# Which feed-forward prepares the rounding remainders of two mixers' weights

## The chip, the cores and the metric

The kernel runs on one core of a Trainium2 chip. The metric is the device time of one execution in microseconds, as the median of several. The core has a matrix engine (PE, TensorE), two elementwise engines (DVE is VectorE, ACT is ScalarE), a general one (POOL, GpSimd) and a queue that only issues transfers here (SP, SyncE). The trace lists when each instruction ran, what it waited for and which clock the matrix engine was granted.

## The reference

A sequence of 512 positions of width 1024 passes through seven layers with a residual sum, each on an RMS-normed input. In short:

```python
x = x + 0.5 * swiglu(rms(x), w_ffn1)                # f1
x = x + mixer1(rms(x))                              # m1: recurrence, window attention
x = x + 0.5 * swiglu(rms(x), w_ffn2)                # f2
x = x + rms(even_mixer(rms(x), w_in_even, w_out_even))   # e: short convolution, dilated attention
x = x + rms(conv_ffn(rms(x), w_up0, w_down0))       # f3
x = x + rms(odd_mixer(rms(x), w_in_odd, w_out_odd)) # o: long convolution, stick-breaking attention
x = x + rms(conv_ffn(rms(x), w_up1, w_down1))       # f4
```

Everything is float32. The even mixer has an input matrix of 1024 x 3072 and an output matrix of 1024 x 1024, the odd one 1024 x 2560 and 1024 x 1024. The feed-forwards have 2816 hidden units, a gate and an up part each; conv_ffn adds a causal convolution of 3 taps on the gate.

## The kernel before

**Three products for one.** The matrix engine reads rounded float32 (`fp32r`). Each weight and each activation is therefore cut in two: `hi`, the value rounded by a cast on ACT, and `lo`, the remainder `raw - hi`, by a subtraction on DVE. `mm3` (L168) makes three matmuls of them: whi*xhi, wlo*xhi, whi*xlo (L170, L171, L172), each 128x128 weights by 512 (or 256) columns. A weight tile of 128x1024 thus gives 24 matmuls.

**How a weight tile comes in.** `wload` (L107) issues one 512 KB transfer into `raw` (3 buffers), casts it to `whi` on ACT (L132) and subtracts on DVE into `wlo` (L139); `whi` and `wlo` have 3 buffers each. Where the source is a `Split` (L37), a pair of DRAM tensors, the subtraction is left out and `wlo` is loaded by a second transfer from the second tensor (L137), issued on SP like the first.

**Who writes that second tensor.** `presplit` (L144) is a generator. Its first step swaps the entry in `ins` for a `Split`; each step handles one tile of 128x1024: load it into one of the 3 `raw` buffers (L151), twice cast a half to a temporary (L155) and subtract in place (L156), then store the tile to DRAM (L157). `ffn` (L418) takes such a generator as `extra=(generator, steps)` and advances it after each of its 22 hidden tiles `j`, so that `steps` steps are spread over the up phase (L455 to L458). For each `j` the up phase has two weight tiles (gate into PSUM kind "m", up into "o"), 48 matmuls, the gate's scaling, optional convolution (L446 to L450), SiLU (L451), the product (L453) and its split (L454). Then comes the down phase (`finish`, L213).

**Stages.** `build` (L1156) runs f1, m1, f2, e, f3, o, f4. Before the change `presplit` of `w_in_odd` (20 tiles) and `w_out_odd` (8 tiles) runs in f2; only the odd mixer reads a `Split`. The even mixer (L866) loads 24 tiles of `w_in_even` and 8 of `w_out_even`, all cut by ACT and DVE. It starts with `begin` (L192), which loads five tiles and runs their products on each half of the columns as soon as that half is normed; then it weaves the projections of four head pairs (`unit`), the short convolution (`gated`) and attention steps (`attention`, L482), and ends with `out_proj` (L965), four of whose eight tiles go to buffers of their own (`oh`, `ol`). In an attention step DVE adds the bias and takes the row maximum (L579), ACT the exponential (L581), DVE the reciprocal and the scaling (L583, L584), PE transposes (L511), ACT and DVE split the result (L514, L515), and PE multiplies by the values (L527).

**What sets the order.** The program is written tile by tile; a planner lays out the order of instructions on each engine beforehand from priorities (program order) and modelled durations, and places the waits. On the chip each queue runs in that fixed order. SP's queue holds every transfer of the kernel: a load that waits for its buffer holds up all loads behind it.

Of the kernel before, what the change touches and what calls it, by code (L numbers as in the profile page):

```python
# [19 lines left out]
KD = D // P  # L20
# [1135 lines left out]
def build(tc, ins, out, stages=STAGES):  # L1156
    with ExitStack() as ctx:
        n = Net(ctx, tc, ins)
        n.out = out
        n.early = stages[0] != "f1"  # L1160
        if n.early:
            n.consts()
        if n.early:
            n.first_prep(PREP[stages[0]])
            n.prep(PREP[stages[0]], WHOLE)
        for s, t in zip(stages, [*stages[1:], "end"]):
            nxt = PREP.get(t, ("end",))
            if s == "f1":
                n.ffn(ins["w_ffn1_gu"], ins["w_ffn1_down"], nxt)
            elif s == "m1":  # L1170
                n.mixer1(nxt)
            elif s == "f2":
                extra = n.chain(n.presplit("w_in_odd"), n.presplit("w_out_odd"))
                n.ffn(ins["w_ffn2_gu"], ins["w_ffn2_down"], nxt, extra=(extra, 28))
                for _ in extra:
                    pass
            elif s == "e":
                n.even(nxt)
            elif s == "f3":
                n.ffn(ins["w_up0"], ins["w_down0"], nxt, conv=("w_fc", "b_fc", 0), post=("norm_g", 3 * KD))  # L1180
            elif s == "o":
                n.odd(nxt)
            elif s == "f4":
                n.ffn(ins["w_up1"], ins["w_down1"], nxt, conv=("w_fc", "b_fc", 1), post=("norm_g", 7 * KD))
# [139 lines left out]
```

## Time and profile before

| | us |
|---|---|
| median of 3 runs | 2469.83 |
| lowest and highest | 2468.75, 2471.17 |
| the profiled execution | 2468.92 |
| its span, first to last instruction | 2467.1 |

Busy time is given per engine over the span. A matmul's printed duration overlaps with the next one's, so that the distance from one start to the next, or the number of matmuls in a stretch, tells more than busy time. In the trace f2 has its up phase until about 1105 us, the even mixer runs from about 1239 to 1490 us, f3 from there to about 1838 us with its up phase until about 1720 us, and the odd mixer from there to about 2110 us.

### The profile page before, as it was taken

Reading aid. Unit: us, or ns where it says so; the run is one execution under the profiler, and the core shown is the slowest. Engines: PE = TensorE matmul, PEld = TensorE weight load, DVE = VectorE, ACT = ScalarE, POOL = GpSimd, SP = SyncE. Lnnn points to the kernel's source line nnn. Section 1 sums busy time; section 2 is a strip of 40 time slices with the busy share of each in tenths; the row PEclk is TensorE's granted clock in tenths of the full one; section 3 lists DMA queues with packets and bytes.
Section 4 is the critical chain, followed back from the end, with each engine's and each line's share of the span. In section 5 each row is a group of like instructions: output and inputs, shape, how many; then the busy total and the mean of one; then the engine's idle time right before and its main releaser. Section 6 shows DMA issues by size and latency. Waiting matters only on the chain.

```text
span 2467.1 us, 32225 instructions
## 1 busy us (share of the span) xinstructions
PE 2401.1 (97%) x12710; PEld 2046.1 (83%) x12710; DVE 1474.5 (60%) x2524; ACT 1129.3 (46%) x1849; POOL 38.8 (2%) x75
## 2 busy tenths in 40 slices
PE   9999999999999999999999999999999879999998
PEld 8888898777777798888988798888898759888887
DVE  5444347888888755553566665554358985655434
ACT  5223236766666544442355554333246556433322
POOL 0000000000000000000000000000001120000000
PEclk9999999999999999999999999999999999999999
DMA  4232333322222256663432222223354313232232
GB/s 151 94 103 92 94 112 119 96 88 88 79 100 84 86 203 213 215 225 98 116 120 90 77 95 77 94 94 98 95 166 152 127 54 136 69 100 97 90 99 92
DMA packets 83560, 276.10 MB, mean 112 GB/s; under 512 B 9328, under 2 KB 14064, under 8 KB 83408
## 3 DMA queue, kind: packets, MB, share of 16 engines
q1 hardware_dynamic: 83408, 274.03, 34.2%
q8 instruction: 100, 1.64, 0.3%
q14 instruction: 52, 0.43, 0.1%
HBM read 257.20 MB, written 16.80 MB: 111 GB/s over the span
## 4 chain that ended last, share of the span: by engine, by line
PE 83%; DVE 10%; ACT 5%; issue 1%; DMA 1%; POOL 0%; SPq 0%; ACTq 0%; DVEq 0%; POOLq 0%
PE psm L172 15%; PE psm L170 15%; PE psm L171 15%; PE pso L170 10%; PE pso L171 10%; PE pso L172 10%; ACT whi L132 1%; DVE wlo L139 1%; DVE pso L1058 1%; PE pst L511 1%; PE pso L527 1%; PE pst L278 1%; PE pst L170 1%; PE pst L172 1%; PE pst L171 1%
## 5 line engine op out<-in xcount | busy, mean ns | idle before, releaser
L132 ACT CAST whi<-raw 128x1024 fp32r<-128x1024 f32 (+3 forms) x402 | 408.4, 1017 | 755.8 <-issue 332.5
L139 DVE TENSOR_TENSOR wlo<-raw,whi 128x1024 fp32r<-128x1024 f32 (+2 forms) x380 | 447.6, 1179 | 311.1 <-ACT whi L132 309.9
L170 PE MATMUL psm<-hh,whi 128*128 128x512 f32 (+1 forms) x1512 | 572.9, 379 | 4.0 <-ACT hh L321 2.8
L171 PE MATMUL psm<-hh,wlo 128*128 128x512 f32 (+1 forms) x1512 | 569.0, 376 | 0.0
L172 PE MATMUL psm<-hl,whi 128*128 128x512 f32 (+1 forms) x1512 | 568.8, 376 | 0.0
L170 PEld LDWEIGHTS psm<-hh,whi 128*128 128x128 f32 x1512 | 285.8, 189 | 53.9 <-ACT hh L321 3.9
L172 PEld LDWEIGHTS psm<-hl,whi 128*128 128x128 f32 x1512 | 285.6, 189 | 49.1 <-DVE hl L322 0.4
L171 PEld LDWEIGHTS psm<-hh,wlo 128*128 128x128 f32 x1512 | 286.4, 189 | 46.0
L170 PE MATMUL pso<-hh,whi 128*128 128x512 f32 (+1 forms) x728 | 272.5, 374 | 0.9 <-ACT whi L132 0.9
L172 PE MATMUL pso<-hl,whi 128*128 128x512 f32 (+1 forms) x728 | 272.3, 374 | 0.0
L171 PE MATMUL pso<-hh,wlo 128*128 128x512 f32 (+1 forms) x728 | 272.2, 374 | 0.2 <-DVE wlo L139 0.2
L171 PE MATMUL psm<-mh,wlo 128*128 128x512 f32 (+1 forms) x506 | 172.4, 341 | 1.6 <-DVE wlo L139 1.6
L172 PE MATMUL psm<-ml,whi 128*128 128x512 f32 (+1 forms) x506 | 172.0, 340 | 0.0
L170 PE MATMUL psm<-mh,whi 128*128 128x512 f32 (+1 forms) x506 | 172.0, 340 | 0.0
L170 PEld LDWEIGHTS pso<-hh,whi 128*128 128x128 f32 x728 | 137.8, 189 | 25.0 <-ACT whi L132 1.1
L172 PEld LDWEIGHTS pso<-hl,whi 128*128 128x128 f32 x728 | 137.7, 189 | 24.6 <-issue 0.5
L171 PEld LDWEIGHTS pso<-hh,wlo 128*128 128x128 f32 x728 | 137.7, 189 | 24.4 <-DVE wlo L139 0.5
L453 DVE TENSOR_TENSOR md<-pso,gp 128x512 f32<-128x512 f32 x84 | 58.1, 692 | 164.2 <-PE pso L172 162.7
L171 PE MATMUL pso<-mh,wlo 128*128 128x256 f32 (+1 forms) x440 | 145.6, 331 | 1.3 <-DVE wlo L139 1.3
L170 PE MATMUL pso<-mh,whi 128*128 128x256 f32 (+1 forms) x440 | 145.8, 331 | 0.3 <-ACT whi L132 0.3
L172 PE MATMUL pso<-ml,whi 128*128 128x256 f32 (+1 forms) x440 | 145.7, 331 | 0.0
L171 PEld LDWEIGHTS psm<-mh,wlo 128*128 128x128 f32 x506 | 96.6, 191 | 12.7 <-DVE wlo L139 2.2
(293 smaller groups left out, 3764.1 us busy)
## 6 DMA issues: line engine op xcount, KB each, us to landing
raw<-w_up SPq DMA_DIRECT2D x88, 512.0 KB, 3.3
raw<-w_ffn_gu SPq DMA_DIRECT2D x87, 512.0 KB, 3.4
raw<-w_in SPq DMA_DIRECT2D x56, 512.0 KB, 3.3
raw<-w_ffn_down SPq DMA_DIRECT2D x40, 512.0 KB, 3.5
raw<-w_in_odd SPq DMA_DIRECT2D x40, 512.0 KB, 3.9
raw<-w_down SPq DMA_DIRECT2D x38, 512.0 KB, 3.5
raw<-w_in_even SPq DMA_DIRECT2D x24, 512.0 KB, 3.5
w_in_odd_lo<-raw SPq DMA_DIRECT2D x20, 512.0 KB, 3.0
```

The lines of the kernel that those rows point to most:

```text
L132: nc.scalar.copy(hi, raw[:, c])
L139: nc.vector.tensor_tensor(out=lo, in0=raw[:, c], in1=hi.bitcast(F32), op=ALU.subtract)
L170: nc.tensor.matmul(out, w[0], x[0], start=start, stop=False)
L171: nc.tensor.matmul(out, w[1], x[0], start=False, stop=False)
L172: nc.tensor.matmul(out, w[0], x[1], start=False, stop=stop)
L278: self.nc.tensor.matmul(st[:, b : b + 1], sq[:, i * P : (i + 1) * P], self.ones[:, 0:1], start=new and i == 0, stop=True, skip_group_check ...
L453: nc.vector.tensor_tensor(out=md, in0=pu, in1=gp, op=ALU.mult)
L511: nc.tensor.transpose(pt[:, i * P : (i + 1) * P], p[:, i * P : (i + 1) * P], self.ident)
L527: nc.tensor.matmul(o[:, q0:q1], V[:, g, a].rearrange("p i d -> p (i d)"), p[:, c], start=first, stop=g == 3 and p is pl, skip_group_check= ...
L1058: nc.vector.scalar_tensor_tensor(t, pad[:, i : i + S], w(i), t, ALU.mult, ALU.add)
```

## The change

`presplit` of the odd mixer's matrices moves from f2 to f3, and f2 now prepares the even mixer's matrices in the same way. The even mixer then reads a `Split`, so its 32 tiles are loaded as two transfers each and are cast on ACT but not subtracted on DVE. f2 advances 32 steps in place of 28, f3 28 in place of none. A loop after f2 that used up what is left of the generator goes; 32 is the number of its tiles (24 + 8), as 28 is for the odd mixer (20 + 8).

```diff
             elif s == "f2":
-                extra = n.chain(n.presplit("w_in_odd"), n.presplit("w_out_odd"))
-                n.ffn(ins["w_ffn2_gu"], ins["w_ffn2_down"], nxt, extra=(extra, 28))
-                for _ in extra:
-                    pass
+                extra = n.chain(n.presplit("w_in_even"), n.presplit("w_out_even"))
+                n.ffn(ins["w_ffn2_gu"], ins["w_ffn2_down"], nxt, extra=(extra, 32))
             elif s == "e":
                 n.even(nxt)
             elif s == "f3":
-                n.ffn(ins["w_up0"], ins["w_down0"], nxt, conv=("w_fc", "b_fc", 0), post=("norm_g", 3 * KD))
+                extra = n.chain(n.presplit("w_in_odd"), n.presplit("w_out_odd"))
+                n.ffn(ins["w_up0"], ins["w_down0"], nxt, conv=("w_fc", "b_fc", 0), post=("norm_g", 3 * KD), extra=(extra, 28))
```

## Rows read from the trace of the kernel before

**Rows 1.** Page, part 1: busy time, share of the span, instructions by engine.
```profile
PE 2401.1 (97%) x12710; PEld 2046.1 (83%) x12710; DVE 1474.5 (60%) x2524; ACT 1129.3 (46%) x1849; POOL 38.8 (2%) x75
```
**Rows 2.** Stretches in f2, f3: length, busy PE, PEld, DVE, ACT, POOL, clock, DMA.
```profile
950.00:1100.00 150.00, 150.00 (x664) 124.20 (x663) 81.00 (x104) 62.81 (x90) 0.00 (x0) 1.00 0.64 221
1550.00:1700.00 150.00, 150.00 (x664) 124.24 (x663) 80.16 (x97) 54.02 (x68) 0.00 (x0) 1.00 0.30 98
```
**Rows 3.** The same view: even mixer between its begin and its tail.
```profile
1250.00:1440.00 190.00, 187.20 (x1004) 157.55 (x1004) 120.71 (x254) 104.81 (x205) 0.13 (x2) 1.00 0.30 98
```
**Rows 4.** PE's waits, 1250 to 1440 us: total us, times, longest.
```profile
PE pst L511 <- DVE l L584: 2.5, 6, 0.6
```
**Rows 5.** DVE's subtractions of weights, 1228 to 1440 us: busy, mean ns.
```profile
L139 DVE TENSOR_TENSOR wlo<-raw,whi 128x1024 fp32r<-128x1024 f32 (+1 forms) x33 | 39.7, 1206 | 16.9 <-ACT whi L132 16.6
```
**Rows 6.** Timelines of DVE, then PE, at an attention step: start us, duration.
```profile
1315.75 1.23 DVE L139 TENSOR_TENSOR wlo<-raw,whi 128x1024 fp32r<-128x1024 f32 x1
...
1318.17 0.39 PE L171 MATMUL psm<-hh,wlo 128*128 128x512 f32 x1
1318.81 0.44 PE L511 MATMUL pst<-ident,l 128*128 128x128 f32 x2 [0.25 <-DVE l L584]
```
**Rows 7.** The chain that ended last, where it passes a subtraction before a transpose.
```profile
1279.15 1.23 DVE wlo L139
...
1352.48 1.23 DVE wlo L139
```
**Rows 8.** Timelines of ACT, then PE, before the other kind of wait.
```profile
1324.22 0.72 ACT L581 ACTIVATE l<-l,m 128x512 f32<-128x512 f32 x1
...
1326.12 0.63 PE L511 MATMUL pst<-ident,l 128*128 128x128 f32 x4 [0.55 <-DVE l L584]
```
**Rows 9.** Page, part 5: the halves that presplit casts and subtracts, 28 steps.
```profile
L156 DVE TENSOR_TENSOR raw<-raw,hi 128x512 fp32r<-128x512 f32 x56 | 36.5, 687 | 41.2 <-ACT hi L155 41.2
L155 ACT CAST hi<-raw 128x512 fp32r<-128x512 f32 x56 | 32.0, 616 | 52.1 <-DMA raw<-w_in_odd 33.1 <-DMA raw<-w_out_odd 19.0
```
**Rows 10.** ACT's waits in f2's up phase, 885 to 1100 us.
```profile
ACT hi L155 <- DMA raw<-w_in_odd: 29.9, 11, 5.6
ACT whi L132 <- DMA raw<-w_ffn_gu: 12.7, 4, 5.2
```
**Rows 11.** Timelines of ACT, then DVE, in f3's up phase: one weight tile.
```profile
1602.24 1.05 ACT L132 CAST whi<-raw 128x1024 fp32r<-128x1024 f32 x1 [1.01 <-PE pso L172]
1603.33 1.23 DVE L139 TENSOR_TENSOR wlo<-raw,whi 128x1024 fp32r<-128x1024 f32 x1 [0.37 <-ACT whi L132]
```
**Rows 12.** Page, part 6: transfers, count, size, median us from issue to landing.
```profile
w_in_odd_lo<-raw SPq DMA_DIRECT2D x20, 512.0 KB, 3.0
wlo<-w_in_odd_lo SPq DMA_DIRECT2D x18, 512.0 KB, 3.4
```
**Rows 13.** Even mixer's begin: ACT's timeline, then PE's.
```profile
1237.23 1.05 ACT L132 CAST whi<-raw 128x1024 fp32r<-128x1024 f32 x1 [1.16 <-PE pso L172]
...
1239.27 0.28 PE L171 MATMUL psm<-hh,wlo 128*128 128x256 f32 x1
```
**Rows 14.** PE's waits at the odd mixer's begin, 1815 to 1865 us.
```profile
PE pso L170 <- ACT whi L132: 1.2, 2, 0.9
```
**Rows 15.** SP's waits in the odd mixer, 1865 to 2035 us.
```profile
SPq L137 <- PE pso L527: 32.4, 1, 32.4
```
**Rows 16.** PE's timeline at the end of the even mixer's last attention.
```profile
1414.17 0.28 PE L527 MATMUL pso<-pl,v 128*128 128x128 f32 x1
...
1414.80 0.39 PE L171 MATMUL pso<-yh,wlo 128*128 128x512 f32 x1
```
**Rows 17.** Stretches, columns as in Rows 2: even mixer's tail, f3's begin.
```profile
1485.00:1490.00 5.00, 2.86 (x24) 2.57 (x22) 3.93 (x9) 2.51 (x5) 0.00 (x0) 1.00 0.63 203
1491.00:1496.00 5.00, 5.00 (x32) 5.00 (x31) 4.04 (x6) 3.77 (x5) 0.00 (x0) 0.66 0.14 56
1496.00:1501.00 5.00, 5.00 (x44) 5.00 (x43) 2.74 (x5) 1.92 (x4) 0.00 (x0) 1.00 0.01 3
```

## The prediction

> **What bounds the kernel now.** I read the busy time by engine first: PE works in 97% of the span [rows 1], so an edit on DVE, ACT or SP counts only where PE waits for it. A busy PE may still be a slow one, because printed durations overlap; the second view, stretches with the number of matmuls, settles that. In f2, with presplit running beside it, PE finishes 664 matmuls in 150 us; in f3, without presplit, also 664 [rows 2]. That is 0.226 us for one of 512 columns in both. So the up phases run at PE's own pace, and twenty-eight steps of presplit cost PE nothing there.
>
> The third view is the stretch of the even mixer, which the change is to relieve. Between its begin and its tail PE is idle for 190.00 - 187.20 = 2.8 us while DVE is busy for 120.7 of 190 [rows 3]. This is the first number that decides: whatever DVE is spared here, it can give back little more than that. The view of waits names the cause: 2.5 of the 2.8 us are the transposes of the attention waiting for DVE's scaled row, six times [rows 4]. The chain of waits and the timelines then show what stands in front of that row. In three of the six a weight subtraction of 1.23 us does [rows 6, 7]. In the others the row follows straight on ACT's exponential, which comes late in ACT's own queue [rows 8].
>
> **The change, part by part.**
>
> **The even mixer loses its subtractions.** That is 32 tiles at 1.21 us [rows 5], 38.6 us of DVE. Off the path it is worth nothing. On the path it is worth the three waits. I size one by starts: from 1318.17 to 1318.81 is 0.64 us, where 0.226 is usual, so 0.41 us is lost [rows 2, 6]; the printed idle time is 0.25 because a matmul's modelled end overlaps. The subtraction in front is three times as long as the wait, so all of the wait goes: 3 x 0.41 = 1.2 us. After that the next in line is ACT's chain, which the change leaves alone, as all casts stay. Ends: at least the printed idle time, 3 x 0.25 = 0.75 us; at most all waits of the stretch at the same ratio, 2.8 x 0.41 / 0.25 = 4.6 us. I take 1.2, since the other waits have ACT before them [rows 8].
>
> **It gains 32 second transfers on SP.** A second part lands 3.4 us after issue [rows 12], where the subtraction took 1.2. Inside the mixer this lies beside other work: there are three buffers, so one that comes free is read again two tiles later, and two tiles are 48 x 0.226 = 10.8 us of PE, more with attention between them. At the begin the cover is thinner. The second tile's buffer comes free at about 1237.2, when the cast into its partner starts [rows 13]; a load issued then lands at 1240.6. PE enters the first tile at about 1239.2 [rows 13] and needs 24 matmuls of half width, 24 x 0.113 = 2.7 us, before the second: 1241.9. It fits by 1.3 us. No trace of the even mixer shows such loads. The odd mixer has them and there PE waits 1.2 us at its begin, for a cast [rows 14]; that is the upper end, and a begin that is freed of DVE work by as much is the lower, -1.2. I take 0, because the arithmetic of the even mixer's own rows leaves no wait.
>
> **f2 gets four more steps.** One step is 2 x 0.687 us of DVE, 2 x 0.616 of ACT [rows 9], one load and one store on SP. The rows of f2 carry 28 already at full pace [rows 2]: 0.
>
> **f3 gets all 28.** This is 38.5 us of DVE and 34.5 of ACT, over an up phase of 22 x 48 x 0.226 = 239 us. In the 150 us stretch DVE goes from 80.2 to 80.2 + 38.5 x 150 / 239 = 104 us, ACT from 54.0 to 76 [rows 2]. Neither becomes the bound. The cover is delay, not share: in f3 a buffer is free at 1602.2, its cast and subtraction are done at 1604.6 [rows 11], and PE wants it 10.8 us after it came free, so there are 10.8 - 2.4 = 8.4 us to spare. What presplit adds is waiting in ACT's queue. In f2 a cast of presplit waited up to 5.6 us for its load, and a weight cast up to 5.2 for its own [rows 10]; both are under 8.4, and PE lost nothing. The traffic of f3 should rise from 98 to about the 221 GB/s of f2 [rows 2]; it did not hurt there. I take 0. Without the cover it would cost what the third rival pays.
>
> [...]
>
> **The odd mixer** reads the same tensors as before. Their stores now end with f3's up phase, some 100 us ahead of its first load: 0.
>
> **Sum.** -1.2 us. Against the profiled execution, whose span is 2467.1 and whose time is 2468.92, that gives 2467.7. The median of the three runs, 2469.83, stands 0.9 above that execution, so the forecast for the median is 2468.6 us. A change of 0.2% is 4.9 us, about what a measurement of this kernel can tell from none; the forecast is a quarter of it.
>
> **The rivals.**
>
> First, the gain is larger. With DVE at some 43% in the even mixer (120.7 - 38.6 of 190), the planner may lay its order anew so that all waits go: -4.6. And the tail of the mixer may shorten. [...] Together -6.0: 2463.8 us. Against it: half of the waits hang on ACT [rows 8], and no subtraction of an even weight is left in the tail.
>
> [...]
>
> Second, SP becomes the hindrance at the even mixer's output, and the time rises. Four of the eight output tiles go to buffers of their own, which come free only when the last attention is done. In the odd mixer, which already works in this way, SP stood 32.4 us at one second-part load, waiting for just that product [rows 15]. In the even mixer this product ends at 1414.45, and PE wants the second output tile's `wlo` at 1414.80 [rows 16]. If that tile's load stands behind the blocked one, it lands at 1414.45 + 3.4 = 1417.9 and PE loses 3.1 us; with the begin's upper end, 4.3. Less the 1.2 gained, that is +3.1: 2472.9 us. It decides from the planner's order: only if SP has the load for a buffer of its own before that for the second tile. For it speaks the 32.4 us; against it that the odd mixer lists no wait of PE for a transfer in that place.
>
> Third, f3's cover breaks. Six of the 22 hidden tiles get two steps. If in each of them two waits of 5.6 us add up, a weight is 11.2 - 8.4 = 2.8 us late, 6 x 2.8 = 17 us: 2485 us. It decides from 8.4 us of delay. Against it: f2 has the same six doubled tiles, with PE at full pace. For it: f3's tile has three more operations in the chain (L448 to L450).
>
> Fourth, the change does nothing: the even mixer would go on subtracting. The entry is swapped at the first step in f2, long before the mixer reads it, and 32 steps cover 32 tiles, so I see no way to that: 2469.8.
>
> **How the numbers follow.** Forecast 0.62, larger gain 0.15, SP 0.15, f3 0.06, nothing 0.02. The predicted time is that of the likeliest, 2468.6. The range runs from the larger gain, 2463.8, to SP's price with the spread of the runs above the median (1.3) on it, 2474.2; outside lie f3, and the far ends of the other two. Faster by over 0.2%: most of the first rival and a little of the forecast's own upper end, 0.16. Slower by over 0.2%: f3, and SP where more than one tile is late, 0.15. Within: 0.69.
>
> **What would show it.** In the changed profile f3 should again have 664 matmuls in 150 us, with L155 and L156 beside them, and PE no wait in f2 or f3. The even mixer should have no L139 on its own weights, and DVE near 43%. The waits of the transposes should fall from six to three, those that are left with ACT in front. PE should wait for no second part at 1240 or at 1415, and the low clock behind the tail should stay. The prediction is wrong if PE's count in f3 falls, if PE waits for a transfer in the even mixer, or if the odd mixer, which the sum holds unchanged, takes another time.

## The result, and the profile after

The changed kernel takes 2482.8 us in the median of five executions, against 2469.9 for the kernel before beside it: a ratio of 1.0052 with a 95% interval of 1.0041 to 1.0063. It became 12.9 us slower, where the forecast was 2468.6 and the range ended at 2474.2. Three of its five executions have a mean granted clock of 0.987 or 0.988 and take 2482.8 to 2486.8 us, two have 0.991 or 0.992 and take 2478.0 and 2478.9; the profiled one took 2486.46 us, at 0.987.

Page, part 1, answers [rows 1]. PE has the same instructions, and the engines that the change was to relieve are not less busy: DVE is where it was, since 32 long subtractions became 64 half ones in f2, and ACT has 34 us more.

```profile
PE 2412.3 (97%) x12710; PEld 2053.4 (83%) x12710; DVE 1474.6 (59%) x2556; ACT 1163.4 (47%) x1913; POOL 38.9 (2%) x75
```

**Where it went.** PE runs the same number of matmuls, so the k-th of one trace can be set against the k-th of the other. The table gives how much later the k-th starts, by stage, for the profiled execution of each run (bounds at 880, 1125, 1262, 1440, 1512, 1720 us of the kernel before, and 1870 to 2112 us for the odd mixer; what lies between is 0 to 1.5 in all). Medians are over all of a run's executions; one execution each of e8 (2957 us, mean granted clock 0.748) and e16 (2657 us, 0.843) ran far slower, and the ratios leave it out.

| run | f2 up | f2 down, e begin | e middle | e tail | f3 up | odd | median, us |
|---|---|---|---|---|---|---|---|
| changed | 5.2 | 1.8 | 1.3 | 4.3 | 0.0 | 5.1 | 2482.8 |
| changed, again | 5.5 | 0.5 | 0.9 | 3.3 | 0.0 | 4.9 | 2481.3 |
| before, again | 0.0 | 2.9 | 0.0 | -0.1 | 0.0 | 0.0 | 2470.8 |
| e1 f3's part alone | 0.0 | 0.1 | -0.1 | 4.1 | 0.0 | -0.2 | 2473.3 |
| e2 even in f2, odd in f1 | 4.1 | 0.3 | 1.8 | -0.1 | 0.0 | 5.0 | 2483.9 |
| e3 24 steps in f2 | 0.0 | 0.0 | 0.4 | 3.2 | 0.0 | 3.4 | 2475.3 |
| e4 buffers of their own in f2 | 4.4 | 0.0 | 3.8 | 3.4 | 0.0 | 3.5 | 2485.2 |
| e5 f3 from tile 5 | 7.6 | 0.5 | 0.8 | 0.8 | 0.0 | 4.9 | 2483.0 |
| e6 28 in f2, 4 behind | 0.0 | 21.7 | 1.1 | 1.4 | 0.0 | 0.6 | 2495.6 |
| e7 w_in_even in f1, kl on DVE | 0.0 | 0.5 | 1.0 | 1.2 | 0.0 | -0.1 | 2472.3 |
| e8 before, kl on DVE | 0.0 | 0.3 | 0.2 | -0.1 | 0.0 | 0.0 | 2469.8 |
| e9 f2's steps one by one | 0.0 | 1.0 | 2.0 | 3.0 | 0.0 | 5.1 | 2476.5 |
| e10 and f3's, from tile 5 | 0.0 | 0.3 | 2.1 | -0.1 | 0.0 | 5.1 | 2478.5 |
| e13 changed, L1115 on DVE | 0.9 | 0.5 | 0.9 | 2.0 | 0.0 | 1.3 | 2480.2 |
| e14 before, L1115 on DVE | 0.0 | 0.4 | -0.1 | 0.8 | 0.0 | 0.6 | 2472.2 |
| e15 e14, no taps on GpSimd | 0.0 | 0.5 | -0.2 | -0.1 | 0.0 | 3.9 | 2473.7 |
| e16 e10, L1115 on DVE | 0.0 | 0.6 | 1.6 | 1.1 | 0.0 | 1.2 | 2473.8 |

Two executions of the kernel before agree within 0.1 us in every column but that of the even mixer's begin. What stands in that column up to 2.9 is therefore no finding by itself. The tail's column has its own spread too: e7, in which f3 prepares nothing, has 1.2 there.

**f2's up phase.** Stretches of the changed kernel answer [rows 2]: in f2 649 matmuls in 150 us in place of 664, in f3 again 664, with L155 and L156 beside them.

```profile
950.00:1100.00 150.00, 148.09 (x649) 121.23 (x648) 77.65 (x102) 60.53 (x88) 0.00 (x0) 1.00 0.65 222
1550.00:1700.00 150.00, 150.00 (x664) 124.26 (x663) 100.72 (x133) 72.51 (x105) 0.00 (x0) 1.00 0.60 216
```

Its waits in f2, PE's from 860 to 1120 us (total, times, longest), then ACT's and SP's from 885 to 1125 us, answer [rows 10]:

```profile
PE psm L171 <- DVE wlo L139: 2.0, 4, 0.7
PE pso L171 <- DVE wlo L139: 0.9, 2, 0.5
```
```profile
ACT hi L155 <- DMA raw<-w_in_even: 46.3, 12, 7.4
ACT whi L132 <- DMA raw<-w_ffn_gu: 36.9, 11, 4.5
```
```profile
SPq L118 <- DVE wlo L139: 68.6, 20, 6.0
SPq L151 <- DMA w_in_even_lo<-raw: 26.7, 10, 4.3
```

PE waits for weights, and the weights wait for their loads, 36.9 us in 11 waits where it was 12.7 in 4. One number shows how it builds up: the time from the end of a weight's subtraction to the first matmul that reads it, worked out from DVE's and PE's timelines. Two tiles of the changed kernel, DVE and PE each time:

```profile
935.81 1.23 DVE L139 TENSOR_TENSOR wlo<-raw,whi 128x1024 fp32r<-128x1024 f32 x1 [0.40 <-ACT whi L132]
...
945.63 0.39 PE L171 MATMUL pso<-hh,wlo 128*128 128x512 f32 x1
...
1048.09 1.23 DVE L139 TENSOR_TENSOR wlo<-raw,whi 128x1024 fp32r<-128x1024 f32 x1 [2.75 <-ACT whi L132]
...
1049.37 0.50 PE L171 MATMUL psm<-hh,wlo 128*128 128x512 f32 x1 [0.22 <-DVE wlo L139]
```

In quiet tiles this distance is 8.6 us. In the kernel before it dips to 5.4 and comes back. In the changed one it reads 8.6 at 946 us, 5.4 at 978, 4.2 at 989, 2.0 at 1022, 0.1 at 1049, and from there it swings between 0.1 and 2.1.

**The even mixer's begin.** PE waits for a second part at the mixer's first weight tile, behind one matmul. The wait and, of three second parts that SP issues there, the shortest, median and longest time from issue to landing:

```profile
PE psm L171 <- DMA wlo<-w_in_even_lo: 1.8, 1, 1.8
```
```profile
DMA to landing us min/median/max: 5.3/5.9/6.4
```

The first of them is issued at 1239.35 us and is the one that took 6.4. In the repetition the wait is 0.4 us, in e2, e5, e7, e9, e10, e13 and e16 it is 0.2 to 0.9; e3 and e4 have none.

**The even mixer's middle** answers [rows 3] and [rows 4]. DVE has 92 us of work in place of 121, and PE gained nothing: there are four waits of the transposes left, and one new wait of 1.0 us for ACT.

```profile
1250.00:1440.00 190.00, 186.50 (x993) 155.48 (x992) 91.77 (x234) 105.62 (x206) 0.13 (x2) 1.00 0.55 178
```
```profile
PE pst L511 <- DVE l L584: 1.9, 4, 0.6
PE psm L170 <- ACT yh L164: 1.0, 1, 1.0
```

**Its tail.** SP's timeline, then ACT's, of the changed kernel: the loads and stores of `presplit`'s first steps of f3 (L151, L157) stand in the tail, ahead of f3's own `w_up`, and their casts (L155) between those of the norm.

```profile
1470.65 5.34 SPq L151 DMA_DIRECT2D raw<-w_in_odd  x3
1477.20 5.17 SPq L157 DMA_DIRECT2D w_in_odd_lo<-raw  x3
1482.42 1.49 SPq L118 DMA_DIRECT2D raw<-w_up  x2
```
```profile
1491.22 0.62 ACT L155 CAST hi<-raw 128x512 fp32r<-128x512 f32 x1 [2.02 <-DMA raw<-w_in_odd]
1491.75 0.90 ACT L321 ACTIVATE hh<-x,vecs 128x256 fp32r<-128x256 f32 x2
```

In the kernel before SP has only `w_up` there:

```profile
1462.94 25.48 SPq L118 DMA_DIRECT2D raw<-w_up  x6
```

ACT waits 2.02 us for a load of the odd mixer's weights, and behind it in its queue stands L321, the activation that PE needs next. PE's waits in the tail (1445 to 1520 us, then the same stretch before) show it, 1.8 in place of 0.3 us:

```profile
PE psm L170 <- ACT hh L321: 1.8, 1, 1.8
```
```profile
PE psm L170 <- ACT hh L321: 0.3, 1, 0.3
```

The rest of the 4.3 us lies beside a lower clock. Right behind, the granted clock is 0.83 over 20 us (0.91 before), and 0.91 over the 20 ahead of that (1.00 before). That part differs from execution to execution: e6 and e13 have the same wait of 1.8 us and lose 1.4 and 2.0 us there.

### The profile page after: what moved, and what is told of

The parts are those of the page before. It is cut to its first block, busy times and chain, and to the rows that moved or that the text cites. A ratio compares the mean times of both kernels' runs of the same rounds, so it can differ in the third digit from the quotient of the medians.

```text
span 2484.7 us, 32485 instructions
## 1 busy us (share of the span) xinstructions
PE 2412.3 (97%) x12710; PEld 2053.4 (83%) x12710; DVE 1474.6 (59%) x2556; ACT 1163.4 (47%) x1913; POOL 38.9 (2%) x75
## 4 chain that ended last, share of the span: by engine, by line
PE 78%; DVE 10%; ACT 6%; DMA 5%; issue 1%; SPq 0%; POOL 0%; ACTq 0%; DVEq 0%
PE psm L172 14%; PE psm L171 14%; PE psm L170 14%; PE pso L171 9%; PE pso L170 9%; PE pso L172 9%; ACT whi L132 2%; DVE wlo L139 2%; PE pst L511 1%; DMA raw<-w_out_even 1%; DVE pso L1058 1%; PE pso L527 1%; PE pst L170 1%; PE pst L171 1%; PE pst L172 1%
## 5 line engine op out<-in xcount | busy, mean ns | idle before, releaser
L139 DVE TENSOR_TENSOR wlo<-raw,whi 128x1024 fp32r<-128x1024 f32 (+2 forms) x354 | 416.0, 1176 | 326.7 <-ACT whi L132 325.7
L156 DVE TENSOR_TENSOR raw<-raw,hi 128x512 fp32r<-128x512 f32 x120 | 79.1, 687 | 55.9 <-ACT hi L155 55.6
```

Of the source, the lines that this page charges most:

```text
L139: nc.vector.tensor_tensor(out=lo, in0=raw[:, c], in1=hi.bitcast(F32), op=ALU.subtract)
L156: nc.vector.tensor_tensor(out=low[:, c], in0=raw[:, c], in1=hi.bitcast(F32), op=ALU.subtract)
```

## The experiments

**e1: f3's part alone.** Odd's 28 steps in f3, nothing in f2, the even mixer cuts its own weights.

```diff
-                extra = n.chain(n.presplit("w_in_even"), n.presplit("w_out_even"))
-                n.ffn(ins["w_ffn2_gu"], ins["w_ffn2_down"], nxt, extra=(extra, 32))
+                n.ffn(ins["w_ffn2_gu"], ins["w_ffn2_down"], nxt)
```

> Only the move to f3: the odd mixer's 28 steps run in f3, f2 prepares nothing, the even mixer subtracts on DVE as before. Theory: about 4 us are lost in the even mixer's tail, because the planner pulls f3's first steps ahead into it, where their casts and subtractions stand in the norm's chain on ACT and DVE; f2 and the even mixer's begin lose nothing; 2474 us, plus up to 6 where the odd mixer is granted the lower clock for longer. Rival: the tail is late because of the even mixer's second transfers on SP; then the tail loses nothing here and the time is that of before, 2470 us.

2473.3 us, ratio 1.0014 [1.0005, 1.0024]. The tail loses 4.1 us and no other stage anything. So the tail's loss has nothing to do with the even mixer's second parts; it comes with f3's steps.

**e2: the even mixer's part with the odd one's elsewhere.** 32 steps in f2, the odd mixer's 28 in f1.

```diff
-                n.ffn(ins["w_ffn1_gu"], ins["w_ffn1_down"], nxt)
+                extra = n.chain(n.presplit("w_in_odd"), n.presplit("w_out_odd"))
+                n.ffn(ins["w_ffn1_gu"], ins["w_ffn1_down"], nxt, extra=(extra, 28))
```

(and f3 without its steps)

> The even mixer's 32 steps in f2 as in the change, the odd mixer's 28 in f1, so that f3 has none. Theory: f2 loses 5 us and the even mixer's begin 1.8 as in the change, its tail nothing, f1 nothing for 28 steps: about 2476 us. Rival (second transfers make the tail late): the tail loses 4 here too: 2480 us.

2483.9 us, ratio 1.0058 [1.0043, 1.0073]. The tail is free of loss, f2 still loses 4.1: the two are separate. f1 carries 28 steps at 0.0. The median lies above both times that I gave: the odd mixer loses 5.0 us here too, though f3 prepares nothing for it, and in e1, where f3 prepares all of it, it loses nothing.

**e3: 24 steps.** `w_out_even` stays with DVE.

```diff
-                extra = n.chain(n.presplit("w_in_even"), n.presplit("w_out_even"))
-                n.ffn(ins["w_ffn2_gu"], ins["w_ffn2_down"], nxt, extra=(extra, 32))
+                extra = n.chain(n.presplit("w_in_even"))
+                n.ffn(ins["w_ffn2_gu"], ins["w_ffn2_down"], nxt, extra=(extra, 24))
```

> As the change, but f2 prepares only w_in_even, 24 steps; the 8 tiles of w_out_even are subtracted on DVE. Theory (three raw buffers carry 28 steps beside the weight loads and not 32): f2 loses nothing, begin 1.8 and tail 4 stay: 2476 us, plus up to 6 from the odd mixer's clock. Rival (each step costs its share of DVE, ACT or memory traffic): f2 loses 24/32 of 5.1, 3.8 us: 2480 us.

2475.3 us, ratio 1.0021 [1.0012, 1.003]. f2 loses nothing, and its distance never falls below 7.5 us. A price per step would have left three quarters of the loss. The even mixer gains nothing from 24 subtractions less.

**e4: buffers of their own.** `presplit` in f2 loads into two buffers that the weights don't use.

```diff
-            raw = self.wp.tile([P, 1024], F32, name="raw", tag="raw", bufs=3)
+            if self.own is not None:
+                raw = self.own.tile([P, 1024], F32, name="sraw", tag="sraw", bufs=2)
+            else:
+                raw = self.wp.tile([P, 1024], F32, name="raw", tag="raw", bufs=3)
```

> As the change, with all 32 steps in f2, but there presplit loads into two buffers of its own and leaves the three raw buffers to the weights. Theory (the shared buffers are what runs out): f2 loses nothing; begin and tail stay: 2476 us, plus up to 6 from the odd mixer's clock. Rival (DVE, ACT or traffic): the same work is there, f2 loses 5 again: 2481 us and more.

2485.2 us, ratio 1.0065 [1.005, 1.008]; f2 loses 4.4. This expectation missed. With buffers to spare the planner drew the steps together, one to some 5.6 us, and now ACT's queue was the place. Its waits from 885 to 1060 us, where L158 is the cast of `presplit`:

```profile
ACT hi L158 <- DMA sraw<-w_in_even: 52.6, 18, 5.4
```

So e4 doesn't tell whether the shared buffers are what runs out in the changed kernel, as the planner's order changed with them. What stayed is that casts wait for their loads ahead of weights' casts.

**e5: f3's steps from its hidden tile 5 on**, 28 over 17 tiles.

```diff
-                        gen, steps = extra
-                        for _ in range(steps * (j + 1) // KF - steps * j // KF):
+                        gen, steps, j0 = (*extra, 0)[:3]
+                        i, n = j - j0, KF - j0
+                        for _ in range(steps * (i + 1) // n - steps * i // n if i >= 0 else 0):
...
-                n.ffn(ins["w_up0"], ins["w_down0"], nxt, conv=("w_fc", "b_fc", 0), post=("norm_g", 3 * KD), extra=(extra, 28))
+                n.ffn(ins["w_up0"], ins["w_down0"], nxt, conv=("w_fc", "b_fc", 0), post=("norm_g", 3 * KD), extra=(extra, 28, 5))
```

> As the change, but f3's 28 steps begin only behind its hidden tile 5, so 28 steps stand over 17 tiles (1.65 a tile) in place of 22 (1.27). f2 and the even mixer are untouched. Theory (the planner lays f3's first steps into the tail of the even mixer): nothing is near enough to the tail to be pulled there, so the 4.1 us that the changed kernel loses between 1445 us and f3's begin go to 0 to 0.7. Rival (the tail is lost to the second parts of w_out_even, or to the planner's other order without subtractions): the 4.1 us stay. Second question, the rate: f2 with 32 steps has 1.45 a tile and loses 5 us. If the rate decides, f3 at 1.65 loses in its up phase as well, by the same slope 2 to 6 us, and the total stays near the changed kernel's 2482.8; if it was f2 alone that couldn't carry more (its tiles have no convolution, but its loads are the same), f3 loses nothing and the total is near 2478.7. f2's 5 us and the begin's 1 to 2 us stay in both.

2483.0 us, ratio 1.0052 [1.0038, 1.0066]. The tail's loss falls to 0.8, and PE's wait for L321 is 0.3 again: the planner had pulled the first steps forward. The second question went against the rate, although the median is the one that I had given to it: that comes from f2, which loses 7.6 here, and the odd mixer. f3 carries 1.65 steps a tile, at more traffic than f2 ever had, with 663 matmuls in 150 us. Eleven of its 17 tiles have two steps, yet the distance from subtraction to matmul dips from 8.6 to 5.7 us there and comes back each time.

```profile
1570.00:1720.00 150.00, 150.00 (x663) 124.21 (x662) 106.24 (x142) 79.17 (x114) 0.00 (x0) 1.00 0.72 261
```

**e6: 28 steps in f2, the last four behind its hidden tiles.**

```diff
-                n.ffn(ins["w_ffn2_gu"], ins["w_ffn2_down"], nxt, extra=(extra, 32))
+                n.ffn(ins["w_ffn2_gu"], ins["w_ffn2_down"], nxt, extra=(extra, 28))
+                for _ in extra:
+                    pass
```

> As the change, but f2 spreads 28 of the 32 steps over its up phase and the last four follow its hidden tiles in a row. Theory (28 steps are carried at full pace, 32 are not): the up phase of f2 loses 0 to 1 us in place of 5; the tail of the even mixer (4 us) and whatever the odd mixer loses stay, so 2475 to 2478.5. Rival (the loss comes from what is prepared, two source matrices of other shapes and other stores, and not from the count): f2 loses 4 to 5 us as before and the total stays at 2481 to 2484. A third outcome, f2's up phase unharmed and 2 to 4 us lost in its down phase or the even mixer's begin, would say that the four steps cost what they cost wherever they stand in one block.

2495.6 us, ratio 1.0114 [1.0098, 1.0129]. f2's up phase loses nothing, with the even mixer's own matrices. The stores tell it too: 24 of them, median from issue to landing 2.9 us here and 4.5 in the changed kernel.

```profile
w_in_even_lo<-raw SPq DMA_DIRECT2D x24, 512.0 KB, 2.9
```
```profile
w_in_even_lo<-raw SPq DMA_DIRECT2D x24, 512.0 KB, 4.5
```

But the four steps landed ahead of the even mixer's weights. SP of e6, then of the kernel before, and PE's wait in e6 from 1240 us on, where it stood still once for 15.7 us:

```profile
1230.93 3.98 SPq L151 DMA_DIRECT2D raw<-w_out_even  x3
...
1256.58 2.05 SPq L118 DMA_DIRECT2D raw<-w_in_even  x2
```
```profile
1230.69 6.99 SPq L118 DMA_DIRECT2D raw<-w_in_even  x4
```

```profile
PE psm L170 <- ACT whi L132: 15.7, 1, 15.7
```

Four steps in one block are the dearest of all. The expectation named this place as a third outcome, but at 2 to 4 us; it cost 21.7.

**e7 and e8: is ACT next in line in the even mixer?** e7 prepares `w_in_even` in f1, leaves the odd mixer's steps in f2, and moves the copies `kl` from ACT to DVE; e8 makes only the last edit, on the kernel before.

```diff
-                QK[m] = q, self.stack_k(ap, self.proj(w_in[16 + m], h, key=("k", m)), 8, nc.scalar.copy)
+                QK[m] = q, self.stack_k(ap, self.proj(w_in[16 + m], h, key=("k", m)), 8, nc.vector.tensor_copy)
```

> Other arrangement: odd's 28 steps stay in f2 as in the kernel before, w_in_even (24 steps) is prepared in f1, f3 prepares nothing, and in the even mixer the four copies kl at L612 run on DVE, which is now freed of 24 subtractions, in place of ACT. Theory: f1 loses 0 to 1 us (24 steps are carried), f2, the tail and the odd mixer lose nothing, and the even mixer gains what the transposes waited, 1 to 2.5 us, because with fewer casts and copies in ACT's queue the exponential comes earlier: 2467 to 2470.5 in all. Rival (sparing DVE and ACT in the even mixer is worth nothing, since the planner fills the place with other work and another wait comes last): 2470 to 2472.

> The kernel before, with the four copies kl (L612) of the even mixer on DVE in place of ACT and nothing else. Theory (three of the transposes' six waits hang on ACT's queue): those three go, 3 x 0.4 = 1.2 us, against up to four new waits on DVE of 0.2 to 0.4 each: 2468.5 to 2470.5. Rival (the waits hang on the order that the planner laid, not on one engine's load): as many waits at other places, 2470 +- 1, and the view of waits names DVE in front of them as before.

e7: 2472.3 us, ratio 1.001 [1.0002, 1.0019]; e8: 2469.8, ratio 0.9999 [0.999, 1.0008]. e7 lies outside the range of the theory and 0.3 us above the rival's; in e8 the time fits both, and the waits decide, six as before. PE's waits for the transposes in the even mixer's middle, in e7 and then in e8, against 2.5 us in [rows 4]:

```profile
PE pst L511 <- DVE l L584: 2.4, 4, 0.8
```
```profile
PE pst L511 <- DVE l L584: 2.7, 6, 0.6
```

e7 takes 24 subtractions off DVE, both move four copies from ACT to DVE, and the waits are as long in all. So they don't follow either engine's load; that they belong to the order that the planner lays fits this, but no run shows it.

**e9 and e10: one step at a time.** The 32 steps of f2 get 44 places, one behind each weight tile, so that no two follow each other. e10 does the same in f3, from hidden tile 5 on.

```diff
                     pg = self.proj(up[2 * j], h, "m", key=(up.tensor.name, 2 * j))
+                    if extra is not None:
+                        advance(extra, 2 * j)
                     pu = self.proj(up[2 * j + 1], h, "o", key=(up.tensor.name, 2 * j + 1))
...
-                        for _ in range(steps * (j + 1) // KF - steps * j // KF):
-                            next(gen, None)
+                        advance(extra, 2 * j + 1)
```

> As the change, but f2's 32 steps are spread over 44 places, one behind each weight tile, in place of 22 (one behind each hidden tile), so that two steps never follow each other directly. Theory (the weights' loads fall behind because ten of 22 hidden tiles have two steps in a row, whose loads and stores hold two of the three raw buffers and each other's transfers back): f2's up phase loses 0 to 1 us in place of 4 to 7.5, its stores land in about 3 us in place of 4.5; the tail's 4 us stay: 2474 to 2479. Rival (32 steps are too many for three buffers and one queue however they are spread): 4 to 7 us lost as before, 2480 to 2486.

> As the run before in f2, and f3's 28 steps too are spread behind single weight tiles, from hidden tile 5 on. If both mechanisms are told rightly (pairs of steps in f2, f3's first steps laid into the even mixer's tail), all the named losses go but about 1 us in the tail and up to 2 at the even mixer's begin, and with no gain in the even mixer it stands at 2471 to 2475. Rival (the losses turn up elsewhere, as the planner's order shifts): above 2477.

e9: 2476.5 us, ratio 1.0028 [1.0017, 1.004]; e10: 2478.5, ratio 1.0034 [1.0022, 1.0046]. f2's loss is gone in both, 663 matmuls in e9's stretch at more traffic:

```profile
950.00:1100.00 150.00, 150.00 (x663) 124.20 (x663) 85.27 (x111) 66.43 (x97) 0.00 (x0) 1.00 0.71 242
```

In e9 the distance goes down to 2.4 us and comes back, though casts of weights wait for their loads as long as in the changed kernel, 37.6 us in 17 waits. The stores of `w_in_even_lo` land in 4.4 us all the same, so their slowness by itself was not what decided; that part of the expectation missed. In e10 the tail's loss is gone as well. Its median lies 3.5 us above my bound, in the rival's range: in its trace the odd mixer loses 5.1 and the even mixer's middle 2.1.

**The changed kernel and the one before, once more.**

> The changed kernel once more, for a second profiled execution. The question is the odd mixer, which took 5 us more in the first one at a lower granted clock, with the same instruction order. Theory (the clock's course there differs from execution to execution and is not set by the change's work): executions lie between 2478 and 2487 with the granted mean between 0.992 and 0.987, and one at 0.991 or above has 0 to 2 us in the odd mixer where one at 0.987 has 5 to 6; up to f3's end the shift against before is the same 11 to 12 us in both. Rival (the change sets it): the odd mixer's 5 us are in every execution, and the spread comes from elsewhere.

> The kernel before once more, for a second profiled execution of it: how far two executions of the same program lie apart by stage. Theory: all stages but those at the lower granted clock (m1, the mixers' ends, the odd mixer) agree within 0.3 us, and the odd mixer may differ by up to 3 us. Rival: other stages differ as much as the 4 to 5 us that are explained here, which would make them noise.

2481.3 us (ratio 1.0044 [1.0027, 1.0061]) and 2470.8. The losses stand at the same places; the odd mixer's 4.9 us are there again in the execution that has a trace, at a mean clock of 0.987. Three others of the changed kernel have 0.991 to 0.993 and take 2480.0 to 2481.9 us, but no trace shows their stages.

**The odd mixer.** Its instructions stand in the same order as before on PE, DVE, ACT and GpSimd. The first place where the two traces part is this, DVE, GpSimd (POOL) and PE of the kernel before:

```profile
1972.30 0.42 DVE L1013 TENSOR_TENSOR_SCAN f<-f,zero 128x128 f32<-128x128 f32 x1 [0.25 <-ACT f L1010]
...
1972.44 1.36 POOL L1115 TENSOR_TENSOR yd<-yd,yp 64x512 f32<-64x512 f32 x1 [6.18 <-ACT b L1011]
...
1974.10 0.30 PE L511 MATMUL pst<-ident,b 128*128 128x128 f32 x1 [0.90 <-DVE b L1014]
```

and of the changed one:

```profile
1984.36 1.38 DVE L1013 TENSOR_TENSOR_SCAN f<-f,zero 128x128 f32<-128x128 f32 x1 [0.25 <-ACT f L1010]
...
1984.17 1.29 POOL L1115 TENSOR_TENSOR yd<-yd,yp 64x512 f32<-64x512 f32 x1 [5.86 <-ACT yd L1114]
...
1987.35 0.30 PE L511 MATMUL pst<-ident,b 128*128 128x128 f32 x1 [2.09 <-DVE b L1014]
```

GpSimd's add starts 0.19 us ahead of the scan instead of 0.14 behind it, the scan takes 1.38 us in place of 0.42, ending 0.28 us behind the add, and PE waits 2.09 us in place of 0.90. The add itself takes 1.36 us behind the scan and 1.29 ahead of it. This, the longer scan behind an add that has begun, is called the collision below; that the add lengthens it is my reading of these rows, and no run shows by what means. Right behind the longer wait, which ends at 1987.35 us, the clock falls: from 1988 us on, in windows of 1 us, it is 0.85, 0.50, 0.50, 0.50. The 80 us from here, before and changed:

```profile
1968.00:2048.00 80.00, 63.83 (x307) 49.72 (x306) 66.85 (x108) 53.66 (x103) 17.75 (x28) 0.96 0.27 88
```
```profile
1980.00:2060.00 80.00, 65.01 (x285) 50.74 (x284) 66.79 (x107) 49.12 (x97) 17.75 (x28) 0.85 0.23 73
```

Over these 80 us the windows of 1 us have a clock of 1.00 or of 0.50, with a value between only where it changes. Added up from them, the lower level of 0.50 holds for 6.8 us before, in one stretch, and for 23.9 us in the changed kernel, in four. To see whether the collision is the cause, e13 (changed) and e14 (before) make the add on DVE; e15 takes the convolution's taps off GpSimd too; e16 is e10 with the add on DVE.

```diff
-                    nc.gpsimd.tensor_tensor(out=yb[z], in0=yb[z], in1=u[z], op=ALU.add)
+                    nc.vector.tensor_tensor(out=yb[z], in0=yb[z], in1=u[z], op=ALU.add)
```

> The changed kernel with the odd mixer's eight adds L1115 on VectorE in place of GpSimd. Theory (GpSimd's add beside VectorE's scan lengthens the scan, PE's wait grows by 1.2 us and tips the granted clock): no scan beside an add is lengthened, the time at the lower clock between 1970 and 2060 us falls from 24 us towards the 7 of the kernel before, and the odd mixer loses 0 to 2 us in place of 5; with f2's 5 to 7 and the tail's 4 us left, 2477 to 2481, and the executions' spread narrows from 8 us to 4. Against it work eight adds of 0.4 to 0.7 us on VectorE, which can cost up to 3 us where PE waits for L1014. Rival (the clock falls there for another reason, the collision is only beside it): lower clock for 20 us or more again, 2481 to 2486.

> The kernel before with the same edit, to price it by itself. Theory: there the add begins behind the scan, which isn't lengthened at that place, so little is gained; eight adds on VectorE cost 0 to 2 us and save as much at other collisions: 2469 to 2472. Rival (GpSimd's adds cost the odd mixer time all over): 2466 to 2468.5.

> The kernel before with neither the eight adds L1115 nor the twelve taps' adds L1054 on GpSimd: three taps of each of four convolutions go to VectorE (twelve more L1058 of 0.74 us = 8.9 us, eight adds of up to 0.7 us = 5.5 us) and ACT loses twelve L1053. Theory (VectorE is what PE waits for in the odd mixer, 22 us of L1014): 14 us more on VectorE cost more than the collisions save, 2471 to 2477. Rival (the collisions of the two engines are the larger part, as a scan of 128 columns takes 0.42 us alone and 1.38 beside an add): 2463 to 2469.

> The changed kernel with every loss mended that was named: f2's steps behind single weight tiles, f3's likewise and from hidden tile 5 on, and the odd mixer's adds on VectorE. Theory: 2470 to 2474, the kernel before within 0.2%, as nothing is gained in the even mixer either. Rival (the odd mixer's loss hangs on something else): 2476 to 2480, as the run without the last edit.

| run | median, us | ratio |
|---|---|---|
| e13 | 2480.2 | 1.0051 [1.0033, 1.0069] |
| e14 | 2472.2 | 1.0006 [0.9997, 1.0015] |
| e15 | 2473.7 | 1.0017 [1.0008, 1.0026] |
| e16 | 2473.8 | 1.0017 [1.0008, 1.0027] |

e16 keeps f2 and f3 mended and is 4.7 us faster than e10: the changed kernel's loss falls from 12.9 to 3.9 us. But the reason is not the one I gave. In the odd mixer e14 gains some 4 us on the kernel before up to 1980 us, with shorter scans (one of 1.39 us takes 0.94); then the clock falls there too, to 0.85 over the same 80 us, and the gain is gone. In e15, which runs no addition on GpSimd from 1964 to 2018 us, the same happens, and the clock is at its lower level from 2000 to 2007 us already. e14, then e15:

```profile
1968.00:2048.00 80.00, 62.59 (x280) 49.67 (x279) 66.54 (x111) 49.55 (x98) 12.01 (x23) 0.85 0.26 85
```
```profile
1964.00:2044.00 80.00, 59.99 (x273) 46.76 (x272) 70.64 (x119) 43.46 (x88) 6.72 (x20) 0.87 0.20 67
```

The median of e13 falls into the theory's range, but its trace has a clock of 0.83 over those 80 us, the rival's sign, and its spread, 2475.0 to 2487.3 us, didn't narrow.

Of the fourteen traces with the add on GpSimd, eight have the collision: the changed kernel, its repetition, e2, e4, e5, e6, e9 and e10, which are those whose f2 prepares all 32 tiles of the even mixer. In seven of them the clock over those 80 us is 0.85; in e6, with a scan of 1.37 us and a wait of 2.12 us, it is 0.96. Of the six without it five have 0.96, and e3 has 0.89. So the lower clock goes with the collision nearly everywhere, but e6 has the collision alone, and e3 and e13 to e16 have the lower clock alone. The collision costs 1.2 us by itself (a wait of 2.09 us in place of 0.90); what decides the clock behind it stays open, and so does why the add starts earlier in those eight.

## Why the prediction was wrong

**"f2 gets four more steps: 0" failed**, by 5.2 us in the profiled execution. I took 28 steps at full pace as proof that 32 run so. Full pace shows only that the cover isn't used up. The cover was 8.6 us, the number that I had from f3 (8.4), and in the kernel before it was already down to 5.4 at times, under the 5.6 us that a cast waited there [rows 10]. With 32 steps in 22 tiles ten tiles have two, with 28 six, and in f2 the cover no longer refills between the pairs. e3 (24), e6 (28) and e9 (32, singly) all lose nothing, the changed kernel, its repetition, e2 and e5 (32 with pairs) lose 4.1 to 7.6. It is a narrow edge: e13 has the same order up to the odd mixer and the same 32 steps, and there the cover reached 0.1 us only at 1092 us and cost 0.9. Nor do pairs by themselves drain it, as f3 of e5 shows. There the stores of the remainders land in 2.7 us, in f2 of the changed kernel in 4.5; e9 has 4.4, but single steps. With the shared buffers, time was lost only where pairs and late stores met, but 28 steps with pairs in f1 of e2 cost nothing with late stores either (4.5 us there), so why f2 can't carry what f3 carries stays open.

**The third rival had a part of the mechanism and the wrong place.** That waits of doubled tiles add up until a weight is late is what f2 shows, though over many tiles and not in each by itself; I gave it 0.06 and to f3 alone, where nothing was lost in the up phase, in any run. I had excluded it for f2 by the rows of 28 steps.

**"f3 gets all 28: 0" was right for the up phase and failed as a step.** 664 matmuls came as predicted, and ACT and DVE stood near the 76 and 104 us that I gave (72.5, 100.7). But I costed the steps where the program writes them. The planner laid the first of them into the even mixer's tail, and there they cost 4.3 us in the profiled execution: 1.5 for L321 and the rest beside a lower clock. I had [rows 17], the tail with PE idle and the low clock of 0.66 behind it, and asked only what might be gained there. e1 and e5 show that it is these steps. What decided is ACT's wait of 2.02 us at L155 with L321 behind it in the queue: the cast starts at 1491.22 us, L321 at 1491.75. I had weighed such waits in ACT's queue against f3's up phase alone.

**The gain of 1.2 us didn't come.** The subtractions in front of the three waits [rows 6, 7] are gone. In the new order each of them is a wait two matmuls earlier: at the second, 1318 us before, 0.64 us from start to start became 0.46 where 0.226 is usual, so 0.41 lost became 0.23. That is a gain of some 0.2 for each, and a new wait for ACT's cast L164 at the output takes 1.0. "So all of the wait goes" was the error: against the matmuls around it the row came some 0.6 us sooner, but the new order also wants it two matmuls, 0.45 us, sooner. e7 and e8 agree, in that sparing an engine shortened no wait. The first rival's argument from DVE's share was worth nothing: it fell to 48%, and no time was gained. Of its 6.0 us, 1.4 stood for a shorter tail, a term that no run shows: in the runs the tail gains at most 0.1 us and loses up to 4.3.

**The second parts on SP: 0 held at the output and failed at the begin.** At the output no wait for one appears, and the second rival falls. At the begin PE waits 1.8 us for one, 0.4 in the repetition, which is a sign of being wrong that I had named. I reckoned with 3.4 us to landing and with the second tile; it was the first tile's part, and it took 6.4 us. What this adds to the whole can't be told, as the kernel before differs from itself by 2.9 there.

**"The odd mixer: 0" failed in the profiled executions**, by 5.1 us. Tensors and order were as I said. The step overlooked that 6.8 us of its 80 already ran at the lower clock of 0.50 before, in a mixer in which PE waits 22.3 us for L1014, and didn't ask whether that would grow. What made it 23.9 us stays open; the collision of scan and add is beside it, and no run shows it as the cause.

**The sum.** For the profiled execution 5.2 + 1.8 + 1.3 + 4.3 + 5.1 and 0.5 in f4 are 18.2 us in starts, against 17.5 in its time (2486.46 - 2468.92); it was 0.6 us ahead when f2 began. The median is 3.7 us lower. f2's part changes from execution to execution; the odd mixer's may too, by the mean clocks, but no trace of the changed kernel shows it. The range was too narrow for the same reason: its bounds stood at two places of the even mixer, and none at a place where work of a moved step could appear.

## What to carry to other kernels

Full pace says nothing of what is left: read how long a loaded tile lies ready before it is used, and how far that dips and whether it refills, before adding filler work beside it. Here it helped to spread such work singly rather than in pairs, and a block of it ahead of a stage's first loads was the dearest. Where a planner lays the order, a moved step can start before the stage that it is written in, so look at the stage before the one that it is written in, above all at its narrow tail.

## What was not expected of the hardware

One scan of 128 columns on VectorE took 0.42 us in the kernel before, where GpSimd's addition started 0.14 us behind it, and 1.38 us in the changed one, where the addition started 0.19 us ahead. The order on these engines is the same in both kernels, and in a kernel's second execution the same of the two comes first. The row of the kernel before names as the add's releaser an instruction of ACT that it doesn't need, so a delay of 0.3 us stays unexplained. And in the odd mixer, where PE waits often (18 times for L1014 in the kernel before), a longer wait and a lower clock don't always go together: e6 has the wait of 2.12 us and a clock of 0.96, while e14 gained some 4 us, and the clock then fell to 0.85 and the gain was gone.
